# Counting the keys of two query tiles on ScalarE instead of VectorE in a top-k threshold search

## The chip, the core and the metric

One core of a Trainium2 chip runs the whole kernel: TensorE (PE in the profile, its weight loads PEld), VectorE (DVE), ScalarE (ACT), GpSimd (POOL) and SyncE (SP), whose queue issues most of the DMAs. The metric is the device time of one execution in microseconds (us); lower is better. The figure to compare is the median of the runs.

## The reference, cut to what matters

The layer takes x (1024 tokens of 1024 values, float32) through one input projection that feeds two token mixers: softmax attention over selected keys (group A) and chunked gated linear attention (group B, "gla"). An output projection and a mixture of experts follow. The change is in the selection of group A. A light indexer gives every query a score for each key, and the 256 best causal keys are kept:

```python
idx_logits = jnp.einsum('bqhd,bsd->bqhs', iqb, ik_f) * IDX_DIM ** -0.5
score = jnp.einsum('bqhs,bqh->bqs', jax.nn.relu(idx_logits), iwb * IDX_HEADS ** -0.5)
causal = key_pos[None, :] <= tb[:, None]
score = jnp.where(causal[None], score, -jnp.inf)
_, idx = lax.top_k(score, topk)          # topk = 256
```

Only the set of kept keys matters for the output. Queries with at most 256 causal keys keep all of them.

## The kernel before, in words

**Tiles.** The 1024 queries are 8 tiles of 128 (t = 0 to 7). Tile t has (t + 1) * 128 causal keys, so tiles 2 to 7 need a selection. Their float32 scores are `acc[t]` (line 235), 128 queries by 384 to 1024 keys, with -2e38 behind the causal edge. `score_sums` (lines 354 to 363) leaves sums for a mean and a deviation on ScalarE, and a bf16 copy of the scores in `mask(t)`, the place where the mask itself will stand later.

**The search.** For each query a threshold v is sought with about 252 keys at or above it (TARGET, line 31). The state of all queries lies in tiles of 128 x 6 (`st`, one column for each tile 2 to 7). `search(it)` (line 494) is called seven times. It counts the keys at or above v, one VectorE instruction per tile (line 500, with the sum over the row in `st["c"]`), and then moves the bracket lo, hi and computes a new v with some 13 small VectorE instructions (lines 502 to 529). Rounds 0 to 4 (NROUND = 5) count on the bf16 copy, rounds 5 and 6 on the float32 scores. `search_end` (line 533) and `make_mask` (line 550, called at lines 760 to 767) then take the last few keys exactly, with GpSimd for the first step of tiles 2 to 6 (line 557) and VectorE for the rest. If any query ends with more than 8 keys still to take (`nbad`, line 540), a slow exact pass behind `tc.If(rv > 0)` (line 777) redoes all tiles.

**What runs beside it.** While the search runs, TensorE works on the projections of group B. `project_steps` (line 259) does 24 matmuls for one token tile into one of two PSUM buffers `pj` (line 150). A buffer comes free when it has been read: for the projection "vr" by ScalarE in lines 401 and 403, and, after the ScalarE steps of lines 404 and 405, by VectorE in line 406. The first vr projection is TensorE's work during the search; behind its eighth tile stands a small matmul (line 469) that takes a `pj` buffer too. ScalarE copies its result (line 470), and one DMA on SP's queue (line 471) spreads it to the DRAM table `skew` for the position bias. Weights of the projections come by DMA into `wr` (line 247) and are split into two parts, on ScalarE (`wh`, line 253) and on GpSimd or VectorE (`wl`, line 254). The gla stages `gla1` and `gla2` (lines 599 and 662) use all engines in between, and the second "qkv" projection follows (line 748).

**What sets the order.** Every engine works through its own queue in order, and waits at the head of it. Within the index stage and from the gla stage of the second half on, TensorE's order is written out by hand. Elsewhere, and for VectorE, ScalarE, GpSimd and SP in this part, the order of the queues is made when the kernel is built by a planner: it plays the program with costs of its own for every instruction and puts next on an engine what is ready in that play, earlier program text first. So the order of a queue follows the planner's times, not those of the chip. The branch at line 777 is a single block: nothing moves across it.

Of the kernel before, what the change touches and what calls it, by code (L numbers as in the profile page):

```python
# [10 lines left out]
F32 = mybir.dt.float32  # L11
F32R = mybir.dt.float32r
F16 = mybir.dt.float16
BF = mybir.dt.bfloat16
I32 = mybir.dt.int32
U8 = mybir.dt.uint8
AF = mybir.ActivationFunctionType
OP = mybir.AluOpType
# [4 lines left out]
P = 128  # L23
S = 1024
D = 1024
NT = S // P
# [6 lines left out]
NROUND = 5  # L33
# [99 lines left out]
def layer(ctx, tc, x, norm1_g, w_in, q_norm_g, k_norm_g, rel_bias, gla_gate_w2, gla_gate_b, gla_out_norm_g, w_out,  # L133
# [3 lines left out]
    V, A, G, T = nc.vector, nc.scalar, nc.gpsimd, nc.tensor  # L137
# [85 lines left out]
    def mask(t, a=0, b=None):  # L223
        o = t * (t + 1) // 2 * P
        return maskb[:, o + a:o + ((t + 1) * P if b is None else b)]
# [126 lines left out]
    st = {n: scp.tile([P, 6], F32, name="st_" + n) for n in ("mean", "sd")}  # L352
# [95 lines left out]
    with tc.manual_schedule(engines={mybir.EngineType.PE}):  # L448
        fill = filler()
        complete = 3  # L450
        for t in range(2, NT):
            while complete < t:
                complete = max(complete, next(fill)[1])
            for room in score_steps(t):
                while room > 0:
                    ns, c = next(fill)
# [19 lines left out]
    srp = p1.enter_context(tc.tile_pool(name="srp", bufs=2, side="left"))  # L476
# [14 lines left out]
    V.tensor_tensor(st["v"], st["sd"], cf[:, CF_ZQ:CF_ZQ + 6], op=OP.mult)  # L491
    V.tensor_tensor(st["v"], st["v"], st["mean"], op=OP.add)

    def search(it):


        for t in range(2, NT):
            j = t - 2
            jk = srp.tile([P, S], BF, name="jb", tag="jb")
            V.tensor_scalar(jk[:, :(t + 1) * P], mask(t) if it < NROUND else acc[t], st["v"][:, j:j + 1], None,  # L500
                            op0=OP.is_ge, op1=OP.add, accum_out=st["c"][:, j:j + 1])
        V.tensor_scalar(gei, st["c"], TARGET, None, op0=OP.is_ge)
        V.tensor_scalar(lti, st["c"], TARGET, None, op0=OP.is_lt)
        if it == NROUND:
            V.memset(st["clo"], 2.0 * S)
            V.memset(st["chi"], 0.0)
        V.copy_predicated(st["lo"], gei, st["v"])
        V.copy_predicated(st["clo"], gei, st["c"])
        V.copy_predicated(st["hi"], lti, st["v"])
        V.copy_predicated(st["chi"], lti, st["c"])  # L510
        if it == NSEARCH - 1:
            return
        if it == 0:
            V.tensor_scalar(st["num"], st["c"], -TARGET, None, op0=OP.add)
            V.tensor_tensor(st["num"], st["num"], cf[:, CF_CS:CF_CS + 6], op=OP.mult)
            V.tensor_tensor(st["num"], st["num"], st["sd"], op=OP.mult)
            V.tensor_tensor(st["v"], st["v"], st["num"], op=OP.add)
            V.tensor_tensor(st["v"], st["v"], st["lo"], op=OP.max)
            V.tensor_tensor(st["v"], st["v"], st["hi"], op=OP.min)
        elif it < NROUND:  # L520
            V.tensor_tensor(st["den"], st["clo"], st["chi"], op=OP.subtract)
            V.reciprocal(st["den"], st["den"])
            V.tensor_tensor(st["w"], st["hi"], st["lo"], op=OP.subtract)
            V.tensor_tensor(st["w"], st["w"], st["den"], op=OP.mult)
            V.scalar_tensor_tensor(st["num"], st["clo"], -TARGET, st["w"], op0=OP.add, op1=OP.mult)
            V.tensor_tensor(st["v"], st["lo"], st["num"], op=OP.add)
        else:
            V.scalar_tensor_tensor(st["num"], st["c"], -TARGET, st["w"], op0=OP.add, op1=OP.mult)
            V.tensor_tensor(st["v"], st["v"], st["num"], op=OP.add)
# [210 lines left out]

    run(gla1(0, 0))
    search(0)
    search(1)
    w = qkv_load(1)
    run(gla1(0, 1))
    for u in range(4):
        run(gla2(0, u))
        project_qkv(1, 2 * u, w)
        project_qkv(1, 2 * u + 1, w)
        if u < 2:  # L750
            search(2 * u + 2)
            search(2 * u + 3)
            run(gla1(0, u + 2))
        elif u == 2:
            search(6)
            search_end()
            run(gla1(1, 0))
# [844 lines left out]
```

## Time and profile before

| | us |
|---|---|
| median of 3 runs | 1119.3 |
| lowest and highest | 1117.56, 1128.18 |
| the profiled execution, its time | 1117.46 |
| its span from first to last instruction | 1115.3 |
| PE busy | 1003.6 |
| DVE busy | 802.3 |
| ACT busy | 651.9 |

The profiled execution lies with the lowest of the runs. Times in rows are microseconds from the start of the span. A timeline row gives start, length, engine, line, operation, output and inputs, and in brackets how long the engine had stood idle before it and what released it. Two instructions of one engine overlap a little, so the cost of one in a busy queue is from its start to the next start, somewhat less than its length. The stage of the change is from about 107 to 177 us.

### The profile page before, as it was taken

The page shows a single profiled execution, that of the slowest core. Times are in us where ns is not written, and L with a number is a line of the kernel's source. Part 1 is how long each engine was busy: PE and PEld are TensorE (multiplying, and loading weights), DVE is VectorE, ACT ScalarE, POOL GpSimd, SP SyncE. Part 2 cuts the span into 40 slices and gives each one's busy share as a digit, 9 for nine tenths or more (in the row PEclk, how much of TensorE's full clock was granted, in tenths as well). Part 3 has the DMA queues.
Part 4 walks back from the last instruction along what each step waited for, and adds up shares of the span by engine and source line. Part 5 has one row for each costly group of instructions (what it writes and reads, how often), then busy time and mean ns, then how long its engine had stood idle before and what let it go on. Part 6 is the DMA issues. An engine that isn't in the chain of part 4 may idle for free.

```text
span 1115.3 us, 17972 instructions
## 1 busy us (share of the span) xinstructions
PE 1003.6 (90%) x5811; PEld 812.6 (73%) x5811; DVE 802.3 (72%) x2159; ACT 651.9 (58%) x1606; POOL 391.4 (35%) x497
## 2 busy tenths in 40 slices
PE   7999983989799899999998999976999999999992
PEld 7899873878678888898886878854666666666551
DVE  6977992774546678887898667674877776787772
ACT  7887530334454666656665443344877676787661
POOL 4611420571241324325443210053444444444321
PEclk9999987898999999999999999987999999999997
DMA  8201025020020301002213249869999999999983
GB/s 245 73 1 31 16 42 82 15 67 10 20 67 20 86 10 49 26 8 74 72 38 105 83 158 374 330 227 274 311 343 339 335 338 308 350 330 347 340 279 45
DMA packets 84077, 174.77 MB, mean 157 GB/s; under 512 B 13913, under 2 KB 45833, under 8 KB 83977
## 3 DMA queue, kind: packets, MB, share of 16 engines
q1 hardware_dynamic: 76808, 147.99, 39.8%
q0 software_dynamic: 7168, 25.56, 10.0%
q8 instruction: 48, 0.79, 0.3%
q14 instruction: 53, 0.43, 0.1%
HBM read 146.66 MB, written 26.87 MB: 156 GB/s over the span
## 4 chain that ended last, share of the span: by engine, by line
PE 40%; DMA 16%; DVE 9%; ACT 4%; issue 3%; POOL 1%; SPq 1%; POOLq 0%; ACTq 0%; DVEq 0%
DMA out_dram<-y,idx 14%; PE pj L266 10%; PE pj L1092 7%; PE po L926 3%; PE tp L915 2%; PE pj L1418 2%; DVE w L1340 2%; PE pj L1419 2%; PE pj L1417 2%; PE mm L1465 2%; PE mm L1113 1%; PE mm L896 1%; PE mm L897 1%; PE tp L823 1%; ACT w L1339 1%
## 5 line engine op out<-in xcount | busy, mean ns | idle before, releaser
L266 PE MATMUL pj<-wh,w 128*128 128x384 f32 (+1 forms) x1152 | 324.9, 350 | 4.7 <-DVE gv L406 3.5
L266 PEld LDWEIGHTS pj<-wh,w 128*128 128x128 f32 x1152 | 213.2, 194 | 13.2 <-DVE gv L406 4.5
L1339 ACT ACTIVATE w<-w 128x512 fp32r<-128x512 f32 x320 | 191.3, 628 | 46.2 <-PE mm L1419 27.6
L1340 DVE TENSOR_TENSOR w<-w,w 128x512 fp32r<-128x512 f32 x283 | 187.4, 700 | 31.3 <-ACT w L1339 28.8
L266 PE MATMUL pj<-wl,w 128*128 128x384 f32 (+1 forms) x576 | 200.8, 349 | 1.1 <-POOL wl L254 1.1
L266 PEld LDWEIGHTS pj<-wl,w 128*128 128x128 f32 x576 | 112.2, 195 | 6.6 <-issue 3.1
L1417 PE MATMUL pj<-w,xT 128*96 128x512 f32 x256 | 105.7, 413 | 0.6 <-ACT w L1339 0.5
L1418 PE MATMUL pj<-w,xT 128*96 128x512 f32 x256 | 102.3, 400 | 2.7 <-DVE w L1340 1.6
L1419 PE MATMUL pj<-w,xT 128*96 128x512 f32 x256 | 102.0, 398 | 0.0
L1092 PE MATMUL pj<-w,mhl 128*128 128x512 f32 x384 | 101.3, 404 | 0.0
L254 POOL TENSOR_TENSOR wl<-wr,wh 128x384 fp32r<-128x384 f32 x58 | 60.1, 1056 | 109.5 <-ACT wh L253 109.4
L1484 POOL DMA_INDIRECT out_dram<-y,idx x30 | 54.7, 1824 | 98.1 <-ACT w L1339 51.8
L890 POOL TENSOR_TENSOR cb<-bt,maskb 128x256 f32<-128x256 f32 (+1 forms) x64 | 43.6, 682 | 111.7 <-DVE mx L901 83.0
L1092 PEld LDWEIGHTS pj<-w,mhl 128*128 128x128 f32 x384 | 69.1, 189 | 13.7 <-issue 0.9
L1340 POOL TENSOR_TENSOR w<-w,w 128x512 fp32r<-128x512 f32 x37 | 50.7, 1369 | 48.4 <-ACT w L1339 47.2
L1465 PE MATMUL mm<-w,hT 128*96 128x512 f32 x128 | 66.1, 598 | 0.5 <-ACT hT L1455 0.5
L904 ACT ACTIVATE z<-z,mx 128x128 f32<-128x128 f32 (+7 forms) x64 | 49.5, 773 | 27.2 <-DVE mx L901 26.9
L253 ACT ACTIVATE wh<-wr 128x384 fp32r<-128x384 f32 (+1 forms) x72 | 33.8, 511 | 39.5 <-DMA wr<-in_w_in_dram 39.0
L1418 PEld LDWEIGHTS pj<-w,xT 128*96 128x96 f32 x256 | 41.9, 164 | 18.5 <-DVE w L1340 3.4
L1417 PEld LDWEIGHTS pj<-w,xT 128*96 128x96 f32 x256 | 44.2, 173 | 15.0 <-ACT w L1339 1.1
L1419 PEld LDWEIGHTS pj<-w,xT 128*96 128x96 f32 x256 | 42.0, 164 | 18.0 <-DVE xT L1431 0.2
L1427 PEld LDWEIGHTS tp<-cf,xg 96*128 96x128 f32 x256 | 40.9, 209 | 15.9 <-issue 9.4
(358 smaller groups left out, 2189.0 us busy)
## 6 DMA issues: line engine op xcount, KB each, us to landing
w<-in_w_exp_gate_dram SPq DMA_DIRECT2D x64, 512.0 KB
w<-in_w_exp_up_dram SPq DMA_DIRECT2D x64, 512.0 KB
w<-in_w_exp_down_dram SPq DMA_DIRECT2D x64, 512.0 KB
wr<-in_w_in_dram SPq DMA_DIRECT2D x80, 128.0 KB
xt<-in_x_dram SPq DMA_DIRECT2D x16, 512.0 KB
mt<-mixd SPq DMA_DIRECT2D x8, 512.0 KB
out_dram<-xt SPq DMA_DIRECT2D x8, 512.0 KB
h2d<-h SPq DMA_DIRECT2D x7, 528.0 KB
```

What stands on the lines that cost most here:

```text
L254: (V if by[kk + k] == "V" else G).tensor_tensor(b, raw[:, k], f32(a), op=OP.subtract)
L266: T.matmul(ps[:, :width], x_, y_[k], start=(k == 0 and i == 0), stop=(k == KC - 1 and i == 2))
L890: G.tensor_tensor(cb[:, :near], bts[p][:, i, 256 - near:], mask(t, far, L), op=OP.add)
L904: A.activation(z[:, :L], z[:, :L], AF.Exp, bias=mn, scale=-1.0, accum_out=mx[:, 3:4])
L1092: T.matmul(ps, lhs[:, k % 4], w[k, c], start=(k == 0 and i == 0), stop=(k == KC - 1 and i == 2))
L1339: A.activation(a, u, AF.Copy)
L1340: (G if engine == "G" else V).tensor_tensor(b, u, f32(a), op=OP.subtract)
L1417: T.matmul(ps, x[0], y[0], start=first, stop=False)
L1418: T.matmul(ps, x[0], y[1], start=False, stop=False)
L1419: T.matmul(ps, x[1], y[0], start=False, stop=last)
L1465: T.matmul(pd[:n], hT0, parts[2 * hf], start=True, stop=False)
L1484: G.indirect_dma_start(out=out[0], out_offset=bass.IndirectOffsetOnAxis(ap=idx[:CAP, e:e + 1], axis=0), in_=y[:CAP], in_offset=None, compu ...
```

## The change

In rounds 0 to 4 the tiles with most keys, t = 6 (896 keys) and t = 7 (1024 keys), are counted on ScalarE: the sign of v - key is summed over the row (a key below v gives 1, a key above it -1), with the threshold as a per-partition bias. From such a sum s over n keys VectorE gets the count of keys above as n / 2 - s / 2 in one instruction of 128 x 2. Tiles 2 to 5 stay on VectorE, and so do all tiles in rounds 5 and 6. A key equal to v counts one half on ScalarE and one on VectorE. GpSimd writes the two constants n / 2 once. The output of the signs goes to a tile "ja" of its own with one buffer.

```diff
+    keys2 = srp.tile([P, 2], F32, name="keys2", bufs=1)
+    for t in range(6, NT):
+        G.memset(keys2[:, t - 6:t - 5], (t + 1) * P / 2)
+
     def search(it):
+        far = range(6, NT) if it < NROUND else ()
+        for t in far:
+            j = t - 2
+            jk = srp.tile([P, S], BF, name="ja", tag="ja", bufs=1)
+            A.activation(jk[:, :(t + 1) * P], mask(t), AF.Sign, bias=st["v"][:, j:j + 1], scale=-1.0,
+                         accum_out=st["c"][:, j:j + 1])
         for t in range(2, NT):
             j = t - 2
+            if t in far:
+                continue
             jk = srp.tile([P, S], BF, name="jb", tag="jb")
             V.tensor_scalar(jk[:, :(t + 1) * P], mask(t) if it < NROUND else acc[t], st["v"][:, j:j + 1], None,
                             op0=OP.is_ge, op1=OP.add, accum_out=st["c"][:, j:j + 1])
+        if far:
+            V.scalar_tensor_tensor(st["c"][:, 4:6], st["c"][:, 4:6], -0.5, keys2, op0=OP.mult, op1=OP.add)
         V.tensor_scalar(gei, st["c"], TARGET, None, op0=OP.is_ge)
```

## Rows read from the trace of the kernel before

**Rows 1.** Windows: length; busy us (instructions) of PE, PEld, DVE, ACT, POOL; TensorE clock, DMA.

```profile
107.27:157.03 49.76, 45.96 (x256) 41.75 (x255) 49.19 (x173) 23.05 (x55) 17.20 (x31) 0.93 0.13 32
157.03:176.40 19.37, 16.89 (x94) 15.12 (x93) 16.21 (x63) 5.63 (x19) 3.91 (x4) 0.82 0.48 66
176.40:193.95 17.55, 0.70 (x5) 0.38 (x3) 0.02 (x1) 0.00 (x0) 0.00 (x0) 0.67 0.51 74
```

**Rows 2.** Timelines of ScalarE, SP's queue and TensorE from the skew write on.

```profile
158.40 0.84 SPq L471 DMA_DIRECT2D skew<-bsk  x1
159.41 34.21 SPq L247 DMA_DIRECT2D wr<-in_w_in_dram  x6
193.95 0.52 ACT L253 ACTIVATE wh<-wr 128x384 fp32r<-128x384 f32 x1 [23.74 <-DMA wr<-in_w_in_dram]
195.25 1.21 PE L615 MATMUL tp<-glT,w 16*128 16x256 f32 x2 [18.15 <-ACT glT L613]
```

**Rows 3.** Timelines: search's last instruction, first mask step, matmul in front of the branch.

```profile
176.27 0.16 DVE L771 CAST nb<-nbad 128x1 f16<-128x1 f32 x1
195.64 1.61 POOL L557 TENSOR_SCALAR b<-acc,st_hi 128x384 f32<-128x384 f32 x1
276.89 0.16 PE L773 MATMUL pj<-ch,nb 128*1 128x1 f16 x1
```

**Rows 4.** TensorE's waits from 107 to 194: total us, times, longest.

```profile
PE pj L266 <- DVE gv L406: 3.5, 2, 2.2
```

**Rows 5.** Timelines of ScalarE, VectorE and TensorE at the first of these two waits.

```profile
115.98 0.42 ACT L405 ACTIVATE gv<-gv 128x256 f32<-128x256 f32 x1
118.92 0.48 DVE L406 SCALAR_TENSOR_TENSOR gv<-pj,rstd,gv 128x256 f32<-128x256 f32 x1
119.46 0.45 PE L266 MATMUL pj<-wh,w 128*128 128x384 f32 x1 [2.18 <-DVE gv L406]
```

**Rows 6.** TensorE's timeline: the second wait, and the matmul of line 469.

```profile
144.32 0.44 PE L266 MATMUL pj<-wh,w 128*128 128x384 f32 x1 [1.36 <-DVE gv L406]
157.03 0.81 PE L469 MATMUL pj<-bsk,rb 32*8 32x384 f32 x2
```

**Rows 7.** Windows around the two waits (columns as in rows 1).

```profile
118.00:127.00 9.00, 7.37 (x38) 6.86 (x38) 8.90 (x34) 5.24 (x12) 2.73 (x6) 0.81 0.00 1
140.00:149.00 9.00, 7.63 (x41) 7.20 (x40) 8.89 (x35) 1.57 (x4) 0.00 (x0) 0.81 0.00 0
```

**Rows 8.** VectorE's timeline, round 4: first count, tiles 6 and 7, end, new threshold.

```profile
148.94 0.62 DVE L500 TENSOR_SCALAR_CACHE_REDUCE jb<-maskb,st_v 128x384 bf16<-128x384 bf16 x1
...
151.87 1.15 DVE L500 TENSOR_SCALAR_CACHE_REDUCE jb<-maskb,st_v 128x896 bf16<-128x896 bf16 x1
...
152.94 1.28 DVE L500 TENSOR_SCALAR_CACHE_REDUCE jb<-maskb,st_v 128x1024 bf16<-128x1024 bf16 x1
154.14 0.09 DVE L500 DVE_READ_ACCUMULATOR jb<-maskb,st_v 128x1 f32 x1
...
156.40 0.17 DVE L526 TENSOR_TENSOR st_v<-st_lo,st_num 128x6 f32<-128x6 f32 x1
```

**Rows 9.** Groups by form of VectorE and ScalarE: busy us, mean ns of one.

```profile
L525 DVE SCALAR_TENSOR_TENSOR st_num<-st_clo,st_w 128x6 f32<-128x6 f32 x4 | 0.7, 164 | 0.1
L904 ACT ACTIVATE z<-z,mx 128x896 f32<-128x896 f32 x8 | 8.3, 1039 | 3.9 <-DVE mx L901 3.9
L904 ACT ACTIVATE z<-z,mx 128x1024 f32<-128x1024 f32 x8 | 9.2, 1149 | 2.9 <-DVE mx L901 2.9
L500 DVE TENSOR_SCALAR_CACHE_REDUCE jb<-maskb,st_v 128x1024 bf16<-128x1024 bf16 x5 | 6.4, 1274 | 0.0
L500 DVE TENSOR_SCALAR_CACHE_REDUCE jb<-acc,st_v 128x1024 bf16<-128x1024 f32 x2 | 2.6, 1280 | 0.0
```

**Rows 10.** ScalarE's loads of function tables in the whole run.

```profile
L142 ACT ACT_TABLE_LOAD x1 | 1.3, 1283 | 0.7 <-PEq L1591 0.7
L1444 ACT ACT_TABLE_LOAD x1 | 1.3, 1283 | 0.0
```

## The prediction

> **What bounds the kernel now.** I read the windows of the search's stretch first, then the waits in it, then the timelines of the engines that the waits name. Up to the matmul of line 469 VectorE is busy 49.19 of 49.76 us, TensorE 45.96 and ScalarE 23.05 [rows 1]: VectorE is full, and ScalarE has half its time free. That makes the edit look good, but the reader should look at the next two windows too. From 157.03 to 176.40 VectorE finishes the search; from there to 193.95 every engine stands still (TensorE works 0.70 of 17.55 us) while the DMA engines are half busy [rows 1]. What ends this pause isn't the search. ScalarE stands 23.74 us at the head of its queue, at one weight copy (line 253) whose load lands late; copies that TensorE needs are behind it, and TensorE waits 18.15 us for one of them [rows 2]. That load was issued on SP's queue just behind the `skew` write of 158.40 [rows 2]. So the chain of this stage is line 469, line 470, the skew write, the load behind it, 193.95. From the write's issue to the release it takes 193.95 - 158.40 = 35.55 us. The search ends at 176.43 [rows 3], in the pause, 17.5 us early.
>
> So VectorE's work counts only by what it does to the time of line 469. In front of that TensorE waits twice for VectorE's line 406, 3.5 us in all [rows 4]: 2.18 and 1.36 us [rows 5, 6]. Around each wait the granted clock is 0.81 over 9 us [rows 7]: a part of the window ran at the lower of its two levels, 1.2 GHz, after TensorE had stood. That costs (1 - 0.81) x 9 = 1.7 us each time, and the two make up the 0.93 of the whole stretch [rows 1], 0.07 x 49.76 = 3.5 us.
>
> **The change part by part.**
> *Removed from VectorE:* the counts of tiles 6 and 7 in five rounds. By their starts they cost 152.94 - 151.87 = 1.07 and 154.14 - 152.94 = 1.20 us [rows 8], 2.27 a round, 11.3 in all.
> *Added to VectorE:* one instruction of 128 x 2 a round. The same operation at 128 x 6 takes 164 ns [rows 9]; five are 0.8 us. Net relief: 10.5 us.
> *Added to ScalarE:* ten sign sums. The trace has no Sign; line 904 has the same shape of work, a per-partition bias and a sum over the row, at 1.04 us for 896 and 1.15 for 1024 [rows 9]: 2.19 a round, 10.9 in all. ScalarE would be busy 34 of 49.8 us and doesn't become the bound. The pair runs beside the four counts left on VectorE, 151.87 - 148.94 = 2.93 us [rows 8]; if both engines start together, it is done first, and the new instruction waits for nothing.
> *The wait that is added:* a sign sum waits at the head of ScalarE's queue for the v of its round, and behind it stand the vr copies (lines 401 to 405), on which line 406 and the `pj` buffer depend. Where ScalarE is idle it costs nothing. Where a pair stands in front of a copy it costs up to 2.19 us less what is covered: at the first wait line 405 ended at 116.40 and TensorE wanted the buffer at 119.46 - 2.18 = 117.28; line 406 takes 0.48 of these 0.88 us [rows 5], so 0.4 us are covered there. I take 0.6 us for the five rounds: one pair in three places would hit a copy, and most behind a buffer that isn't yet wanted.
> *Two constants on GpSimd:* two instructions of one column that wait for nothing, on an engine busy 17.20 of 49.76 us [rows 1]; I cost them at nothing.
> *What the relief is worth at line 469.* At best both waits and both slow stretches go: 2.18 + 1.36 + 2 x 1.7 = 6.9 us. TensorE is then full up to line 469. Without new waits the other end is nothing: VectorE's queue is laid out by the planner, and the search doesn't wait for TensorE, so what the two counts leave free is taken by rounds 5 and 6 pulled forward, and line 406 stands behind as much work as now. The first wait speaks for a gain: line 405 ended at 116.40 and line 406 started 2.5 us later [rows 5], behind the rest of round 0 and two counts of round 1, and round 0 will be 2 us shorter. The second stands further back, where the planner can refill. I take the first with its slow stretch, 2.18 + 1.7 = 3.9 us, less the 0.6: 3.3 us.
> *Behind line 469* all up to 193.95 moves with it as a block. The search ends some 10 us earlier, in the pause, where nothing waits for it. The masks could start in the pause (line 557 runs only at 195.64 [rows 3], behind a weight part on GpSimd's queue that needs the same load). But after the pause TensorE has its own work up to the branch, whose matmul comes at 276.89 [rows 3]; earlier masks are worth nothing, at most the few us that GpSimd's mask steps take from weight parts there.
>
> The profiled execution took 1117.46 us, 2.2 more than its span. Less 3.3 it is 1114.2. The median of the runs shown, 1119.3, is 1.8 above the profiled one; I put the new median at 1115.
>
> One rule speaks against the change. "VectorE: DVE Perf Modes" of the Trainium skill (section "The perf-mode tier table") gives a one-source bf16 operation in SBUF four times the plain rate, and float32 twice. By it the removed counts would be cheap, as an estimate some 0.4 us each, and ScalarE's pair longer than all six of a round. But the counting form takes 1274 ns on bf16 and 1280 on float32 [rows 9]: no such rate. The measurement decides, and the relief stays 2.27 us a round.
>
> **The rivals.**
> *Refilled, nothing gained.* Line 406 stands behind as much work as now, and the relief ends up wholly in the pause. For it: VectorE is busy 99% up to line 469 [rows 1], and the search has more rounds to give. Against it: the first wait comes before there is much to pull forward. Time: 1117 to 1119.
> *The pause shrinks.* One weight copy blocks ScalarE, and its place in the queue is planned. Should the new plan put it behind the copies that TensorE needs, the 18.15 us [rows 2] go. Against it: the planner places that copy by the end of the skew write in its own play, which moves with line 469, so the distance stays. Time: 1117.5 - 18 = about 1100.
> *ScalarE waits at v (slower).* The plan sets the pair where it expects v; VectorE runs later than planned (line 406 came 2.5 us after its input [rows 5]), so ScalarE stands at the sign with the vr copies behind it. It decides where the wait for v plus the pair passes the 0.4 us that are covered. With the whole update in the wait, 156.57 - 154.14 = 2.4 us [rows 8], TensorE loses 2.4 + 2.2 - 0.4 = 4.2 us and 1.7 at the low clock: 5.9 in a round. In two of five rounds that is 11.8: 1129.
> *It doesn't do what it says.* If Sign isn't in the function table that ScalarE holds, each round loads two tables of 1283 ns [rows 10], 12.8 us of ScalarE in front of copies: about 1125. Against it: the whole run has two loads [rows 10], though this half uses Square, Copy, Relu, Abs, Exp and Ln. And a key equal to v counts half; should that leave a query unsolved, the slow pass would run over all tiles, hundreds of us. Rounds 5 and 6 count exactly, so I give that almost nothing.
>
> On tables, "ScalarE: Activation LUTs" of the Trainium skill (section "Table sets: the hidden batching unit") says that cheap functions stand in every set, and puts a switch at about 2.7 us; by that figure ten switches are 27 us. The two loads of this run agree with its first half.
>
> **How the numbers follow.** The forecast, 1110 to 1118: 0.45. Refilled: 0.23. The pause shrinks, wholly or by half: 0.13. ScalarE waits at v: 0.14. Tables or slow pass: 0.05. A measurement of this kernel tells about 1% from no change, 11 us either way. Faster by more: the pause and an edge of the forecast, 0.17. Slower by more: the wait at v and the last rival, 0.15. Between: 0.68. The range runs from 1101, the pause nearly gone, to 1127, the wait at v in not quite two rounds.
>
> **What would show it.** Right: four counts a round on VectorE in rounds 0 to 4, ten sign sums of 1.04 and 1.15 us on ScalarE, line 469 near 154, the weight copy released some 36 us after the skew write as now, the search over near 166, and line 266's waits for line 406 under 1.5 us. Wrong: line 469 at 157 or later (refilled); ScalarE waiting for `st_v` and TensorE's waits above 5 us (the slower rival); or the 18.15 us wait of line 615 gone (the pause).

## The result and the profile after

The changed kernel is slower: a median of 1135.8 us (four runs, 1131.58 to 1139.44) against 1121.6 of the kernel before in the same comparison (a fourth run of it is in), a ratio of 1.0122, interval 1.008 to 1.0164. The profiled execution took 1131.58 us with a span of 1129.5, 14.1 more than the profiled execution of before. The forecast was 1115, and the range ended at 1127. The count of line 500 stands at 513 in the changed kernel, and what is below it 15 lines further down: 607 is 622, 615 is 630, 683 is 698, 726 is 741, 771 is 786.

The two engines did what the edit says. Groups by form of the changed kernel, 107 to 170 us (busy us, mean ns of one | idle before, releaser):

```profile
L506 ACT ACTIVATE ja<-maskb,st_v 128x1024 bf16<-128x1024 bf16 x5 | 5.7, 1136 | 0.0
L506 ACT ACTIVATE ja<-maskb,st_v 128x896 bf16<-128x896 bf16 x5 | 5.2, 1043 | 7.2 <-DVE st_v L541 6.1 <-DVE st_v L492 1.1
L516 DVE SCALAR_TENSOR_TENSOR st_c<-st_c,keys 128x2 f32<-128x2 f32 x5 | 0.9, 177 | 0.1
```

Ten sign sums of 1.04 and 1.14 us and five small instructions of 0.18: the prices of [rows 9] were right. The 7.2 us are idle time in front of the sums: ScalarE stood at the head of its queue for the v of the round.

The windows of the three stretches of [rows 1] in the changed kernel (length; busy us of PE, PEld, DVE, ACT, POOL; clock, DMA):

```profile
107.27:157.03 49.76, 42.38 (x243) 39.50 (x242) 48.59 (x176) 32.48 (x73) 17.42 (x31) 0.93 0.11 29
157.03:176.40 19.37, 16.52 (x101) 14.04 (x100) 9.21 (x35) 5.53 (x19) 5.57 (x5) 1.00 0.50 68
176.40:195.00 18.60, 0.00 (x0) 0.00 (x0) 0.00 (x0) 0.00 (x0) 0.00 (x0) 0.50 0.53 77
```

VectorE is as full as before up to 157 (48.59 of 49.76 us, though 11.3 us of counts are gone), and TensorE has worked 3.6 us less. In the pause nothing runs at all. TensorE's waits in the first stretch, to be set beside [rows 4] (total us, times, longest):

```profile
PE pj L266 <- DVE gv L406: 5.2, 2, 2.6
...
PE mm L690 <- DVE dd L668: 2.1, 1, 2.1
```

The 3.5 us of before have become 7.3. At the first of these waits line 406 comes no earlier than the 118.92 of [rows 5]:

```profile
119.35 0.47 DVE L406 SCALAR_TENSOR_TENSOR gv<-pj,rstd,gv 128x256 f32<-128x256 f32 x1
```

Round 1 starts its counts at 113.78 instead of 117.72, and all four now stand in front of line 406. VectorE's timeline further on shows where the relief ended up:

```profile
168.28 0.16 DVE L786 CAST nb<-nbad 128x1 f16<-128x1 f32 x1
195.74 0.97 DVE L172 TENSOR_TENSOR rs_u<-rs_u,rs_w 128x4 f32<-128x4 f32 x1 [27.31 <-ACT rs_w L167]
...
197.49 1.12 DVE L741 SCALAR_TENSOR_TENSOR o<-mm,ms,gv 128x128 f32<-128x128 f32 x4
```

The search's last instruction comes 8 us earlier than in [rows 3], and then VectorE stands 27 us. What it stands for is on ScalarE's timeline. First the kernel before, behind the skew write; the weight copy of [rows 2] at 193.95 comes next in this queue:

```profile
164.75 0.30 ACT L166 ACTIVATE rs_w<-ms,cf 128x4 f32<-128x4 f32 x1
165.08 0.21 ACT L167 ACTIVATE rs_w<-rs_w 128x4 f32<-128x4 f32 x1
165.19 0.58 ACT L607 ACTIVATE qk<-tp 128x512 f32<-128x512 f32 x1
169.62 0.58 ACT L396 ACTIVATE gq<-pj,rstd 128x384 f32<-128x384 f32 x1 [3.85 <-PE pj L266]
```

And the changed kernel:

```profile
167.04 0.57 ACT L396 ACTIVATE gq<-pj,rstd 128x384 f32<-128x384 f32 x1
167.51 0.30 ACT L166 ACTIVATE rs_w<-ms,cf 128x4 f32<-128x4 f32 x1
195.09 0.52 ACT L253 ACTIVATE wh<-wr 128x384 fp32r<-128x384 f32 x1 [27.29 <-DMA wr<-in_w_in_dram]
195.52 0.19 ACT L167 ACTIVATE rs_w<-rs_w 128x4 f32<-128x4 f32 x1
195.62 0.56 ACT L396 ACTIVATE gq<-pj,rstd 128x384 f32<-128x384 f32 x1
196.08 0.58 ACT L622 ACTIVATE qk<-tp 128x512 f32<-128x512 f32 x1
```

Behind the weight copy now stand the second half of a norm (line 167, the Exp), an evacuation `gq` and the evacuation `qk` (an evacuation copies a result out of PSUM). Two of them, line 167 and `qk`, stood ahead of it before. The `gq` didn't: one `gq` is ahead of the copy and the next one behind it in both kernels. In the kernel before it is this one, directly behind the copy:

```profile
194.38 0.56 ACT L396 ACTIVATE gq<-pj,rstd 128x384 f32<-128x384 f32 x1
```

TensorE's timeline in the changed kernel:

```profile
157.25 0.81 PE L469 MATMUL pj<-bsk,rb 32*8 32x384 f32 x2
...
198.40 1.37 PE L690 MATMUL mm<-dd 64*128 64x64 f32 x8 [24.85 <-DVE o L741]
```

Line 469 came at 157.25 (157.03 in [rows 6]), the skew write at 159.54, the copy's release at 195.09: 35.55 us from write to release, to the hundredth as before. But TensorE stopped at 198.40 - 24.85 = 173.55 and waited 24.85 us, where [rows 2] has 18.15: its PSUM buffer hung on `o` (line 741), `o` on the norm, and the norm's Exp on the weight copy. Up to 195 TensorE had worked 58.90 us since 107.27; the kernel before had 63.56.

From there to attention the distance grows: the first output of attention is written to DRAM at 407.35 instead of 392.96. I use this write as a mark below, since it stands behind all that is in dispute here.

### The profile page after: what moved, and what is told of

Read it like the earlier page. It is cut to its first block, busy times and chain, and to the rows that moved or that the text cites. A ratio compares the mean times of both kernels' runs of the same rounds, so it can differ in the third digit from the quotient of the medians.

```text
span 1129.5 us, 17987 instructions
## 1 busy us (share of the span) xinstructions
PE 1007.7 (89%) x5811; PEld 816.3 (72%) x5811; DVE 798.4 (71%) x2144; ACT 661.8 (59%) x1626; POOL 394.6 (35%) x499
## 5 line engine op out<-in xcount | busy, mean ns | idle before, releaser
L1355 DVE TENSOR_TENSOR w<-w,w 128x512 fp32r<-128x512 f32 x283 | 184.8, 691 | 35.0 <-ACT w L1354 31.3
L266 PEld LDWEIGHTS pj<-wl,w 128*128 128x128 f32 x576 | 112.1, 195 | 5.5 <-issue 3.6
L690 PE MATMUL mm<-dd 64*128 64x64 f32 x256 | 35.6, 327 | 36.2 <-DVE o L741 30.4
L690 PEld LDWEIGHTS mm<-dd 64*128 64x128 f32 x256 | 28.8, 224 | 48.1 <-DVE o L741 31.3
L1433 PEld LDWEIGHTS pj<-w,xT 128*96 128x96 f32 x256 | 42.2, 165 | 21.4 <-POOL w L1355 3.9
L1432 PEld LDWEIGHTS pj<-w,xT 128*96 128x96 f32 x256 | 44.5, 174 | 15.2 <-ACT w L1354 1.3
```

What stands on the lines that cost most here:

```text
L266: T.matmul(ps[:, :width], x_, y_[k], start=(k == 0 and i == 0), stop=(k == KC - 1 and i == 2))
L690: T.matmul(pav[h][:, i, :64].rearrange("p (n s) -> p n s", s=n), dd[rows[h], lv, i], dd[rows[h], lv, i].rearrange("p (n s) -> p n s", s=2 ...
L1355: (G if engine == "G" else V).tensor_tensor(b, u, f32(a), op=OP.subtract)
L1432: T.matmul(ps, x[0], y[0], start=first, stop=False)
L1433: T.matmul(ps, x[0], y[1], start=False, stop=False)
```

## The experiments

The theory: the loss is the order in ScalarE's queue. The new plan set one weight copy, whose load is held up by the skew write, ahead of instructions whose results the other engines want. The rivals: the sign sums themselves cost it in the search's stretch, by ScalarE's waits for v; or the branch behind the masks does, where TensorE stood 3.2 us in the changed kernel's profile instead of 1.2, with a granted clock of 0.83 instead of 0.93 over the 50 us from there.

**The copies held back, in both kernels.** All copies of the second value projection are put behind the last evacuation of the projection in front of it:

```diff
-    w = vr_load(1)
+    with tc.issue_after(last.ins):
+        w = vr_load(1)
```

Expected with the change:

> The changed kernel, with the weight copies of the second value projection held behind the last evacuation of the projection in front of it on ScalarE, so that none of them can stand in front of a norm or an evacuation while its load is behind the skew write. Theory (the order in the pause costs the time): ScalarE no longer stands 27 us at that copy, the norm's Exp of line 167 runs near 168 instead of 195.5, TensorE's wait of 24.85 us in the pause falls under 10, and the time falls by 15 to 22 us, to 1110 to 1120. Rival (ScalarE's sign sums hold up copies in the search's stretch): the pause isn't where the loss is; what the changed kernel loses against its partner without the change stays 12 us or more.

and without it:

> The kernel before with the same hold on the same weight copies. Its pause goes as well: TensorE's 18.15 us wait falls under 10 and the time falls by 8 to 18 us, to 1102 to 1111. Theory: the two kernels so held stand within 5 us of each other, so the sign sums by themselves cost nothing. Rival of the search's stretch: this one is 12 us or more faster than the changed kernel with the hold. Rival of the branch (its 2 us and the low clock behind it are what the change costs): this one is 5 to 8 us faster.

Measured: 0.987 of before (0.9802 to 0.9939) with the change, 0.9872 (0.979 to 0.9953) without, medians 1109.6 and 1110.6 us. The windows of the old pause, first with the change, then without:

```profile
176.40:195.00 18.60, 18.60 (x116) 15.59 (x114) 15.60 (x42) 6.97 (x18) 12.75 (x15) 1.00 0.53 67
```

```profile
176.40:195.00 18.60, 18.60 (x117) 16.13 (x115) 16.07 (x51) 6.17 (x11) 12.83 (x16) 1.00 0.53 81
```

TensorE is full there in both. The skew write still holds up the loads; nothing that is wanted stands behind them. By the medians, of four runs each, the change's loss of 1.2% is gone with the pause, and the rival of the search's stretch, 12 us or more between the two, falls. The rival of the branch, 5 to 8 us, isn't settled by this pair: the medians stand 1 us apart, but the attention marks of the two profiles are 380.62 with the change and 374.66 without, and by the last part of this section two executions of one kernel can differ by as much.

**One exchange each way.** In the changed kernel the copy is held behind line 167 alone:

```diff
+    with tc.issue_after(norm1.ins):
+        w = vr_load(1)
```

> The changed kernel with one exchange in ScalarE's queue: the weight copy that waits for the load behind the skew write is held behind the norm's Exp of line 167 and stands next to it, everything else in the pause as it was. Theory (the exchange of these two is what the change cost): VectorE's line 172 and its `o` run near 170 instead of 196, TensorE's stand in the pause falls from 24.85 us to about 18, and the time falls by 5 to 14 us to the level of the kernel before, 0.995 to 1.006 of it. Rival (the sign sums cost it in the search's stretch, or the branch does by itself): within 3 us of the changed kernel, 1.009 or more.

In the kernel before, the copy is traced early and line 167 is held behind it:

```diff
+        with tc.issue_after(gate[0].ins) if gate and n == 4 else ExitStack():
+            A.activation(w, w, AF.Exp, scale=-0.5)
         ...
+        if u == 0:
+            vr_first(1)
```

> The kernel before, without any sign sum, with the opposite exchange: the first weight copy of the second value projection is traced early and the norm's Exp is held behind it, as the changed kernel's plan has it. Theory: the Exp runs near 194, VectorE's line 172 waits some 27 us, TensorE stands 23 to 26 us in the pause instead of 18.15, and the time rises by 5 to 14 us, 1.005 to 1.013 of before. Rival: no change of the order of these two matters, since the copies that TensorE wants are behind the weight copy in both: 0.997 to 1.003.

Measured: the kernel before with the exchange takes 1.0128 (1.0076 to 1.0179): no sign sum in it, and a loss of the same size. But the way there wasn't the expected one. TensorE stood 16.64 us in the pause, less than 18.15. VectorE stood, in the middle of the search's last round:

```profile
195.33 0.96 DVE L177 TENSOR_TENSOR rs_u<-rs_u,rs_w 128x4 f32<-128x4 f32 x1 [24.00 <-ACT rs_w L170]
```

so that it had 62.72 us of work between 195 and 280 instead of 54.22, and TensorE did 77.97 there instead of 81.42. Nor is all of the loss made there: by the table at the end of this section the router's last write comes 2.7 to 9.5 us later than in the two profiles of the kernel before, and the other 7 to 10 us lie behind it, in the expert stage, whose code nobody touched. So equal size doesn't make it the changed kernel's loss.

The changed kernel with the exchange takes 1.0122 (1.0077 to 1.0166), as much as without it: a miss. Its profile shows what TensorE then stands for:

```profile
196.67 0.69 PE L750 MATMUL tp<-cf,o 128*128 128x128 f32 x2 [22.22 <-ACT qk L624]
```

`qk`, two places behind the copy, took the place of the Exp. (That profiled execution was the fastest of its seven runs, 1124.3 us against a median of 1132.8; its attention mark is 398.57, as in the second profile of the kernel before. So this profile doesn't show the loss that the medians show, and what part of it the Exp alone carries stays open.)

**All three ahead.** The copy is held behind `qk`, so that line 167, `gq` and `qk` all stand ahead of it:

```diff
+    with tc.issue_after(qk_evac[2].ins):
+        w = vr_load(1)
```

> The changed kernel with the weight copy held behind three instructions: the norm's Exp of line 167, the second evacuation `gq` of line 396 and the evacuation `qk` of line 622, so that all that stood ahead of the copy in the kernel before stands ahead of it here. With the Exp alone ahead, TensorE stood 22.22 us for `qk`; theory (what stands behind the copy sets the pause): TensorE's stand falls to 16 to 19 us as in the kernel before, its profile reaches the router's part (the norm's write in front of it, at 751.5 in the kernel before and 766.2 in the changed one) at 748 to 756, and the ratio is 0.993 to 1.005. Rival (sign sums or branch cost the time whatever the order): 1.009 or more.

Measured: 1.0002 of before (0.9964 to 1.0039), median 1120.8. ScalarE's timeline:

```profile
167.02 0.21 ACT L167 ACTIVATE rs_w<-rs_w 128x4 f32<-128x4 f32 x1
169.53 0.58 ACT L396 ACTIVATE gq<-pj,rstd 128x384 f32<-128x384 f32 x1 [2.31 <-PE pj L266]
170.01 0.59 ACT L624 ACTIVATE qk<-tp 128x512 f32<-128x512 f32 x1
194.81 0.52 ACT L253 ACTIVATE wh<-wr 128x384 fp32r<-128x384 f32 x1 [24.21 <-DMA wr<-in_w_in_dram]
```

Up to the copy ScalarE's queue is else that of the changed kernel, instruction for instruction; behind the pause the planner moved a few more (`oT` comes ahead of `zb`). TensorE's wait is longer than the 16 to 19 us expected:

```profile
195.65 1.22 PE L632 MATMUL tp<-glT,w 16*128 16x256 f32 x2 [21.14 <-ACT glT L630]
```

But up to 195 it has worked 62.62 us, close to the 63.56 of before, and VectorE has 51.87 us left between 195 and 280. The attention mark is 394.27, the router's last write 753.03, as expected. All sign sums are still in this kernel, and ScalarE stands 7.3 us at v, as in the changed kernel. So with these three ahead of one copy the whole of the measured loss is gone, and the sign sums, with the relief that pays for them, don't make it. Which of the three carry it isn't told apart; the second `gq` stood behind the copy in the kernel before too.

**The halves of the change.** The load without the relief: ten sign sums added, into a tile that nobody reads, all counts left on VectorE.

```diff
+        for t in range(6, NT) if it < NROUND else ():
+            A.activation(jk[:, :(t + 1) * P], mask(t), AF.Sign, ...
+                         accum_out=junk[:, t - 6:t - 5])
```

> The kernel before with the ten sign sums added on ScalarE, into a tile that nobody reads, and all six counts left on VectorE: the load of the change without its relief. In this plan the norm's Exp stands ahead of the weight copy, as in the kernel before. Theory (order): within 4 us of the kernel before, 0.997 to 1.004, with TensorE's stand in the pause near 18 us. Rival (ScalarE waits at v and TensorE pays in the search's stretch): 5 to 12 us slower, 1.005 to 1.011, with the matmul of the bias rows 3 us or more later than 157.

The relief without the load:

```diff
+    V.memset(st["c"][:, 4:6], TARGET)
     ...
-        for t in range(2, NT):
+        for t in range(2, NT if it >= NROUND else 6):
     ...
+        V.tensor_reduce(nbad, st["w"][:, 0:4], axis=AX.X, op=OP.add)
```

> The kernel before with the counts of tiles 6 and 7 left out of the five rounds on rounded scores, and nothing put on ScalarE: the relief of the change without its load (these two tiles keep a fixed count until the two exact rounds, and the question whether the slow pass is needed is asked of the other four tiles). If VectorE's relief is refilled by rounds pulled forward, line 469 stays at 156 to 158 and the time within 3 us of before, 0.997 to 1.003. If it was the sign sums that ate it, the waits for line 406 shrink, line 469 comes 3 to 7 us earlier, and the time falls by as much, 0.993 to 0.997.

This kernel leaves counts out, so its selection isn't the layer's, and only its time is of use.

Measured: 1.0181 (1.0128 to 1.0234) for the load, 0.9951 (0.9909 to 0.9994) for the relief. Line 469 moves by 8.0 us to 165.05 in the first and by 2.2 us to 154.83 in the second. The stretch of [rows 1] in the kernel with the sums added:

```profile
107.27:157.03 49.76, 40.30 (x216) 37.45 (x214) 47.20 (x156) 29.16 (x64) 15.06 (x28) 0.86 0.10 23
```

TensorE does 5.7 us less by 157, at a lower clock, and waits there:

```profile
ACT ja L501 <- DVE st_v L532: 7.5, 3, 5.9
...
PE pj L266 <- DVE gv L406: 5.3, 2, 3.6
...
PE mm L681 <- DVE dd L659: 2.6, 1, 2.6
```

So ScalarE's stand at v is a real price, and my expectation that this kernel would be level is a miss; in the changed kernel the relief pays for it. It isn't the whole of the 1.8%, though. TensorE's stand in the pause, expected near 18 us, is 23.09, since here too the plan put `qk` behind the copy:

```profile
204.73 0.48 PE L739 MATMUL tp<-cf,o 128*128 128x128 f32 x1 [23.09 <-ACT qk L613]
```

And its expert stage is 10.8 us longer than in the kernel before (this profiled execution was the slowest of its six runs, 1148.8 us against a median of 1144.0). The relief alone, 11.3 us of VectorE's work taken out, is worth some 5 us of 1120. It fits neither expectation whole: TensorE's waits for line 406 stay at 3.5 us, as for refilled, but line 469 comes earlier, and the ratio is in the range of the other.

**The skew write early.** The bias rows' block is put behind the loads of the first value projection, so that the skew write is issued at 113 to 114 instead of 158:

```diff
         w = vr_load(0)
+        bsk = wp.tile([P, 2, 384], F32, tag="wr", name="bsk", bufs=3)
+        ...
+        nc.sync.dma_start(skew, sk[:, None, :].to_broadcast([8, P, 384]))
```

> The changed kernel with the bias rows (their two loads, the matmul, the copy and the skew write) put into the filler right behind the loads of the first value projection, so that the 33 us of the skew write run during the search and no load of the second value projection is behind it. Theory: the copy that blocks ScalarE finds its data there, TensorE waits under 5 us at the end of the search, the pause is gone; 18 to 28 us less, 1105 to 1115. If loads of the projection in front now come late instead, the gain is under 10.

> The kernel before with the same move of the skew write. Theory: its pause goes too, 12 to 20 us less, 1100 to 1107. With no pause left behind the search, what the search takes from VectorE could count, so this is also where the relief of the change might show: the changed kernel with the move would be up to 8 us faster than this one; if the relief is refilled here too, they stand within 4 us.

Measured: 0.984 (0.9768 to 0.9912) with the change, 0.9927 (0.9884 to 0.9971) without; medians 1104.7 and 1113.8 us. Without the change the gain is 8 us by the ratio, short of the 12 to 20 expected. Since the intervals overlap, the pair was run again:

> The changed kernel with the early skew write once more, in more rounds, beside its partner on the same chip. If the relief of VectorE counts where no pause follows the search, this one is faster than its partner by 5 to 10 us in the medians, and the branch's bias loads are issued 6 to 10 us earlier than in the partner (they were at 255.99 and 264.68).

> The kernel before with the early skew write once more. If the first pair's distance was the spread of single executions, the two medians are within 3 us here and the bias loads behind the branch within 3 us of each other.

Measured: 0.9892 (0.9838 to 0.9946) and 0.9932 (0.9895 to 0.997), medians 1105.2 and 1113.5. The medians stand 8 to 9 us apart both times, and the ratios' intervals still overlap. SP's queue in the second pair, with the change and then without (the bias loads behind the branch, attention's first output, the router's last write):

```profile
256.52 0.80 SPq L812 DMA_DIRECT2D bt<-skew  x2
378.94 40.52 SPq L945 DMA_DIRECT2D mixd<-oa  x6
737.17 0.32 SPq L1255 DMA_DIRECT2D h2d<-h  x1
```

```profile
264.48 0.80 SPq L797 DMA_DIRECT2D bt<-skew  x2
377.83 40.49 SPq L930 DMA_DIRECT2D mixd<-oa  x6
737.60 0.32 SPq L1240 DMA_DIRECT2D h2d<-h  x1
```

Both signs of the expectation came: the medians, and the branch 8 us earlier. But at attention's first output the two are level, and they are level at the router's last write; the first pair of profiles says the same (table below). The distance in the profiles arises in the expert stage behind it, 1101.1 - 737.2 = 363.9 us with the change and 1110.6 - 737.6 = 373.0 without, whose code is the same in both. So the signs were met and what they stood for, a relief that lasts to the end, wasn't; why the expert stage differs stays open. Both kernels are faster than the kernel before; the one with the change has the lowest median of all that were run, 1104.7 and 1105.2 us.

**Each kernel again.** For the parts that one profile can't settle:

> The changed kernel once more, for the parts behind the pause. If the plan fixes the loss, its profile shows the same stand of 24 to 26 us in the pause and the branch again more than 3 us for TensorE with a low clock behind it, and the ratio is 1.008 to 1.016. If the branch's 2 us and the clock behind it belonged to that one execution, the branch takes TensorE 1 to 1.5 us here, the clock from 288 to 339 is near 0.92, and the time is 5 to 7 us shorter.

> The kernel before once more, for the spread of its own parts: how far the skew write, the branch and the router's part move between two executions, and how long the expert stage behind the router takes, which was 364 us in some profiles and 371 to 375 in others. If that is a matter of the execution, this profile may have either; if it belongs to a kernel's plan, it is 364 us again.

Measured: 1.0121 (1.0067 to 1.0175) and 1.0028 (0.999 to 1.0065). The pause repeats: TensorE waits 25.02 us for `o`, and has worked 59.45 us up to 195 (63.37 in the kernel before). The branch repeats too. TensorE behind it in the changed kernel, first and second profile:

```profile
290.84 0.66 PE L690 MATMUL mm<-dd 64*128 64x64 f32 x6 [3.23 <-DVE at L698]
```

```profile
284.86 0.66 PE L690 MATMUL mm<-dd 64*128 64x64 f32 x6 [3.18 <-DVE at L698]
```

and in the kernel before:

```profile
281.59 0.66 PE L675 MATMUL mm<-dd 64*128 64x64 f32 x6 [1.19 <-DVE at L683]
```

```profile
281.95 0.66 PE L675 MATMUL mm<-dd 64*128 64x64 f32 x6 [1.41 <-DVE at L683]
```

Over the 50 us from there the clock is 0.83 and 0.80 in the changed kernel, 0.93 and 0.90 in the kernel before. So the 2 us at the branch belong to the plan, as the expectation has it, and not to one execution. In the kernel with all three ahead the wait is 1.33 us and the clock 0.86: the edit that took the loss away took most of this away with it, and the two aren't told apart by it. The wait alone doesn't make a kernel slow: the changed kernel with the early skew write has it too (3.51 and 3.33 us) and has the lowest median of all.

The marks of all profiles, in us (bias loads behind the branch; attention's first output; the router's last write; from there to the end of the span, the expert stage):

| kernel | bias loads | first output | router | expert stage |
|---|---|---|---|---|
| before | 280.85 | 392.96 | 751.48 | 363.8 |
| before, again | 281.20 | 398.61 | 758.21 | 360.4 |
| changed | 288.12 | 407.35 | 766.16 | 363.3 |
| changed, again | 282.13 | 403.60 | 762.95 | 364.9 |
| changed, all three ahead | 279.60 | 394.27 | 753.03 | 363.7 |
| changed, Exp ahead | 280.04 | 398.57 | 756.53 | 365.8 |
| before, Exp behind | 287.25 | 402.21 | 760.94 | 370.6 |
| before, sums added | 294.45 | 412.00 | 771.57 | 374.6 |
| before, counts left out | 275.19 | 389.42 | 748.78 | 364.4 |
| changed, copies held back | 267.68 | 380.62 | 739.88 | 372.1 |
| before, copies held back | 266.05 | 374.66 | 733.62 | 373.9 |
| changed, early skew write | 255.99 | 378.40 | 736.47 | 364.8 |
| the same, again | 256.52 | 378.94 | 737.17 | 363.9 |
| before, early skew write | 264.68 | 378.30 | 737.90 | 371.1 |
| the same, again | 264.48 | 377.83 | 737.60 | 373.0 |

At attention the marks of the kernel before and of the changed kernel differ by 4 to 6 us between two executions (by half a microsecond in the two kernels with the early skew write), and the bias loads of the changed kernel by 6, so a single difference of that size proves nothing. One thing holds in every pair with and without the change: from the bias loads to attention's first output the changed kernel takes longer, by 9 us in both pairs with the early skew write, where there is no pause, by 4 us with the copies held back, and by 2 to 9 us otherwise. With all three ahead this stretch is 114.7 us, within the 112.1 and 117.4 of the kernel before. What sets it wasn't tested.

## Why the prediction was wrong

**Line 469.** I forecast it near 154 and a gain of 3.3 us; it came at 157.25, and at 155.46 in the second profile (157.03 and 157.52 before). The term that failed is the first wait with its slow stretch, 3.9 us. It assumed that line 406 would have 2 us less in front of it; but round 1 was pulled forward into the place of the two counts, line 406 started at 119.35 instead of 118.92, and TensorE waited 5.2 us for it (5.0 in the second profile) and in the first profile 2.1 for `dd`. The rival *Refilled, nothing gained* describes this: VectorE stayed full, and rounds 5 and 6 ended 8 us earlier, in the pause. Its price, about no change, is what the kernel with all three instructions ahead shows, 1.0002 of before. (The sum itself gives 1114.2 for the profiled execution and, with the same 1.8 us on top, 1116.0 for the median; I put 1115.)

**The wait that is added.** I took 0.6 us for it. ScalarE stood 7.2 us at v, and added alone the sums moved line 469 by 8 us. The mechanism of *ScalarE waits at v* was right and stood among the rivals; in the changed kernel it is covered by the relief, and it isn't what made the time longer. The signs that I had named for this rival all came: ScalarE's wait for `st_v`, TensorE's waits above 5 us and a slower kernel. They would have named the wrong cause: in the kernel with all three ahead ScalarE waits as long, TensorE stands 4.6 us for line 406, and nothing is lost.

**Behind line 469.** This is the step that cost the forecast. I wrote that all up to 193.95 "moves with it as a block", and, for the rival *The pause shrinks*, that the planner sets the copy by the end of the skew write, so that the distance stays. The distance did stay, 35.55 us. What didn't stay was which instructions stand in front of the copy, and that wasn't looked at: line 167 and `qk` went behind it, and TensorE's stand grew from 18.15 us (18.91 in the second profile) to 24.85 (25.02). With the three instructions ahead of the copy the ratio falls from 1.0122 to 1.0002. In the kernel before line 167, `qk` and one `gq` are ahead of it and start before 170; the view of ScalarE's queue between 158 and 194 shows them. I had asked only whether the copy would come behind what TensorE needs, which makes the pause shorter, and not whether more would come behind it, which makes it dearer.

**What was right.** The prices of the sums, no table load added, the pause as the place where time can be won or lost, and that VectorE's relief by itself is worth little here.

**What stays open.** How the order becomes 1.2%. TensorE's work up to 195 falls by 3.9 to 4.7 us, the marks behind by 5 to 14 us, and the rest isn't shown. TensorE's stand in the pause alone doesn't rank the kernels: with the Exp alone ahead it is 22.22 us and the ratio 1.0122, with all three 21.14 us and 1.0002, with the counts left out 21.86 us and 0.9951, and in the kernel before with its Exp behind 16.64 us and 1.0128. That the work left to VectorE behind the pause sets the loss is a guess from the last of these kernels, where VectorE had 8.5 us more and TensorE did 3.5 us less. The branch and the stretch behind it carry a part too, and how much of it comes from the order isn't known.

## What to carry to other kernels

When a queue holds one instruction that waits long for a late transfer, its price is all that stands behind it and is wanted sooner: list what is ahead of it and what is behind it before any edit that makes a planner lay the queue out anew. An edit that costs nothing where it is made can lose its time there, and by the medians one ordering edge, or an earlier transfer, was worth more here than the relief of the fullest engine. A sign that a rival predicts isn't proof of the rival: take away the cause and see whether the loss goes. Repeat both profiles before explaining differences of a few microseconds far behind the change, and before dismissing them.

## What the runs showed that I had not expected

The same code behind the router's last write, the expert stage, falls into two groups: 360 to 366 us in nine of the fifteen profiles, 371 to 375 in the other six. Each of the four kernels that were profiled twice is in the same group both times, so it looks like a property of the kernel and not of the execution, though no edit touched that code; the cause is open. Some 5 to 14 us can arise there, as much as the effects under study, far behind the search. Two executions of the kernel before differ by 5.7 us at attention's first output with the same order of instructions.
